# Turning the feed-forward's rows in 32 by 32 squares on VectorE, by way of DRAM, in a hybrid decoder layer

## The chip, the cores and the metric

One Trainium2 chip, of which the kernel uses one core. The metric is the time of one execution on the device in microseconds. The engines are written as in the profile: PE (TensorE, matmuls; PEld is its weight load), DVE (VectorE), ACT (ScalarE), POOL (GpSimd) and SP (SyncE, which here issues the DMAs). Each engine works through its own instructions in the order of the program; semaphores tie them together.

## The reference, cut to what matters

```python
SEQ = 1024; D_MODEL = 1024; D_FF = 4 * D_MODEL

def reference(x, ...):
    h = rmsnorm(x, mix_pre_norm)
    proj = h @ w_in
    ...
    mixed = jnp.concatenate([attn, rec], axis=-1) @ w_out
    x = x + rmsnorm(mixed, mix_post_norm)
    h = rmsnorm(x, mlp_pre_norm)
    ff = jnp.square(jax.nn.relu(h @ w_ff1)) @ w_ff2
    x = x + rmsnorm(ff, mlp_post_norm)
    return x
```

All is float32, with 1024 tokens. The change lies between `@ w_out` and `@ w_ff1`: the rows `h` of the second norm, with tokens on the partitions, have to be turned so that their 1024 features lie on the partitions, as the matmul with `w_ff1` needs them.

## The kernel before

The tokens are worked in NT = 8 blocks of 128 rows. A float32 matmul is made of three passes over a high and a low part of both operands (`three_pass`, lines 90 to 92, and the same in `mm1`, lines 1633 to 1635). `split_into` (86 and 87) makes the parts: ACT copies the high one (names ending in h), DVE subtracts it to get the low one (ending in l). This goes for weights too: `wl` is the low part of a block of FF1's weights, `wa2l` and `wa3l` are those of the second and third pair that FF1 starts with.

A loop over t = 0 to 7 runs the output projection: `late_out(t, 0)` and `late_out(t, 1)` are the matmuls `pwo<-…,mt` of block t. Work on earlier blocks is laid into the same loop by small tables. For a block r it is, in this order: `residual(r)` (DVE, lines 1274 and 1275: the new x, in `xres`, which an SP DMA also writes to DRAM as `x2d`, line 1293), POOL's factor of the norm (`x2r`), `residual_b(r)` (DVE, line 1303: x times factor times gain; the result, the row block of h, lies in `esum` for blocks 0 to 3, in place in `xres` for block 4 and in `x2n` for blocks 5 to 7), and the turn.

The turn is `next_turn(r)`: eight transposes on PE by the identity into two PSUM banks `ph` (line 1313) and two evacuations by ACT (line 1319) into `hraw[kh, th]`. Here kh is the half of the features and th the half of the tokens, so each of the four `hraw` tiles takes parts of four blocks. `TURN_MID` and `TURN_END` say at which t a block is turned. Blocks 6 and 7 come within FF1: `mm1(1, 1, …)` and `mm1(1, 2, …)` call `next_turn` between their matmuls.

`split_tokens` splits the turned tokens of th = 0 into `h2h` and `h2l`, tokens 0 to 255 at t = 5 and 256 to 511 at t = 7. FF1 works by products of halves: `mm1(q, p)` is product p of weight pair q. Products 1 and 2 use th = 0 alone; the others use sums with th = 1 (`B220l`, `T10l` and their like), which are made behind `wa3l` on DVE. FF1 begins with `mm1(0, 1)`, `mm1(1, 1)`, `mm1(0, 2)`, `mm1(1, 2)`, then products 1 of pairs 2 and 3 (`f12a`, `f13a`). Ahead of it SP issues the loads of raw weights: `wr2` and `wr3` (`early_load`) and four `w1r`.

SP issues nearly all DMAs, in order: one that waits for its data holds up all that stand behind it.

Of the kernel before, what the change touches and what calls it, by code (L numbers as in the profile page):

```python
# [8 lines left out]
F32 = mybir.dt.float32  # L9
F32R = mybir.dt.float32r  # L10
# [7 lines left out]
P = 128  # L18
T = 1024
D = 1024  # L20
NK = D // P
NT = T // P
# [15 lines left out]
def hymba_layer(ctx, tc, x, w_in, w_out, w_ff1, w_ff2, g_pre, lb_logits, g_mix, g_post,  # L38
                g_mlp, g_mlp_post, bias_tab, level_masks, ident_in, fold_in, out):
    nc = tc.nc  # L40
    V, S, G, TE = nc.vector, nc.scalar, nc.gpsimd, nc.tensor
# [4 lines left out]
    wide = ctx.enter_context(tc.tile_pool(name="wide", bufs=8))  # L46
# [3 lines left out]
    dp = ctx.enter_context(tc.tile_pool(name="spill", bufs=1, space=DRAM))  # L50

    def slab(tag, name, dtype=F32, shape=(P, T)):
        return sp.tile(list(shape), dtype, tag=tag, name=name,
                       bufs={"S": 9, "T": 9, "P": 3, "BT": 2, "V8": 2, "R": 1}[tag])

    def bank(tag, name):
        return ps.tile([P, 512], F32, tag=tag, name=name,
                       bufs={"mm": 2, "s": 2, "t": 2, "pv": 2}[tag])

    def half(name, dtype=F32):  # L60
        return sp.tile([P, 512], dtype, tag="half", name=name, bufs=2)

    def col(name, n=1):
        return tp.tile([P, n], F32, tag=f"c{n}", name=name)
# [15 lines left out]
    def rsqrt_mean(dst, ssum, n, width):  # L80
        t = col("ms", width)
        G.tensor_scalar(t, ssum, 1.0 / n, EPS, op0=ALU.mult, op1=ALU.add)
        G.tensor_tensor(out=dst, in0=t, in1=nhalf[:, :width], op=ALU.pow)
# [172 lines left out]
    pick32 = cp.tile([P, 32], F32, name="pick32")  # L256
    mix_dram = dp.tile([T, D], F32, name="mixd")
    x2_dram = [dp.tile([P, D], F32, name=f"x2d{t}") for t in range(NT)]

    def ig_evac(hd, pm, blocks):  # L260
        for u, t in enumerate(blocks):
            S.activation(hd["inat"][:, t], pm[:, u, 0], AF.Copy, scale=rstd0[:, t:t + 1])
            V.tensor_scalar(hd["gate"][:, t], pm[:, u, 1], rstd0[:, t:t + 1], None, op0=ALU.mult)
# [873 lines left out]
    rows, xress, mts, pmo, gains, scales = {}, {}, {}, {}, {}, {}  # L1137
# [24 lines left out]
    def early_sum(t):  # L1162
        return early["sum"][t // 2][:, t % 2]
# [82 lines left out]
    def x_again(t):  # L1246
        xress[t] = slab("P", f"xres{t}")
        nc.sync.dma_start(out=xress[t], in_=x[t * P:(t + 1) * P, :])

    def mixed_half(t, hf):  # L1250

        if hf == 0:
            scales["mix", t] = col("pss", 2)
        src = pmo[t, hf]
        if t < NE:
            whole = early_sum(t)[:, hf * 512:hf * 512 + 512]
            V.scalar_tensor_tensor(whole, src, scales["row", t], whole, op0=ALU.mult, op1=ALU.add)
            src = pmo[t, hf] = whole
        S.activation(half(f"dp{t}{hf}"), src, AF.Square, accum_out=scales["mix", t][:, hf:hf + 1])
        if hf == 1:  # L1260
            s2 = scales.pop(("mix", t))
            s1 = col("ps1")
            rp = scales["mix", t] = tp.tile([P, 1], F32, tag="prp", name=f"prp{t}", bufs=2)
            G.tensor_tensor(out=s1, in0=s2[:, 0:1], in1=s2[:, 1:2], op=ALU.add)
            rsqrt_mean(rp, s1, D, 1)

    def residual(t):
        xr = xress[t]
        rp = scales.pop(("mix", t))
        for hf in range(2):  # L1270
            sl = slice(hf * 512, hf * 512 + 512)
            src = pmo.pop((t, hf))
            add = src if t < NE else half(f"ad{t}{hf}")
            V.scalar_tensor_tensor(add, src, rp, gains["gpost"][:, sl], op0=ALU.mult, op1=ALU.mult)
            V.tensor_tensor(out=xr[:, sl], in0=add, in1=xr[:, sl], op=ALU.add)
            if t not in SQ_LATER:
                residual_sq(t, hf)
        if t not in SQ_LATER:
            residual_sq(t, 2)
# [17 lines left out]
    def residual_b(t):  # L1297
        xr = xress[t]
        if t < NE:
            xress[t] = early_sum(t)  # L1300
        elif t >= NT - 3:
            xress[t] = slab("S", f"x2n{t}")
        V.scalar_tensor_tensor(xress[t], xr, scales.pop(("x2", t)), gains["gmlp"], op0=ALU.mult, op1=ALU.mult)

    def next_turn(t):

        xr = xress.pop(t)
        th, c = t // 4, (t % 4) * P
        for kh in range(2):
            pt = bank("t", f"ph2{t}_{kh}")  # L1310
            for j in range(4):
                k = kh * 4 + j
                TE.transpose(pt[:, j * P:(j + 1) * P], xr[:, k * P:(k + 1) * P], ident)
            src = pt.rearrange("p (j c) -> p j c", j=4)
            if t % 4 == 0:
                hraw[kh, th] = wide.tile([P, 4, 512], F32, tag="A", name=f"hraw{kh}{th}")
                if th == 0:
                    h2[kh] = tuple(wide.tile([P, 4, 512], F32R, tag="A", name=f"h2{q}{kh}") for q in "hl")
            S.activation(hraw[kh, th][:, :, c:c + P], src, AF.Copy)

    def split_tokens(kh, c):

        hi, lo = (q[:, :, c:c + 2 * P] for q in h2[kh])
        split_into(hi, lo, hraw[kh, 0][:, :, c:c + 2 * P])
# [50 lines left out]
    for s in range(n_steps):  # L1375
# [19 lines left out]
        kind, g = ITEMS[i]  # L1395
# [51 lines left out]
    h2, hraw = {}, {}  # L1447
# [3 lines left out]
    SCALE = {3: (0,), 4: (1,), 5: (2,), 6: (4,), 7: (5,)}  # L1451
    SCALE_MID = {7: (6,)}
    SCALE_END = {5: (3,)}
    TURN_MID = {6: (3,)}
    TURN_END = {3: (0,), 4: (1,), 5: (2,), 6: (4,), 7: (5,)}

    def scaled(r):
        residual_b(r)
        if r + 3 < NT and r != 4:
            x_again(r + 3)  # L1460

# [5 lines left out]
    for t in range(NT):  # L1467
        late_out(t, 0, last_rows if t == 0 else None)
        for r in SCALE.get(t, ()):
            scaled(r)  # L1470
        if t > 0 and t + 1 < NT:
            for which in range(t + 1 < NE, 2):
                row_turn(t + 1, which, True)
            if t + 4 < NT:
                row_load(t + 4)
        for r in RES_END.get(t - 1, ()):
            for part_ in range(3):
                residual_sq(r, part_)
        if t < 2:
            x_again(t + 1)  # L1480
        if NE <= t + 2 < NT:
            row_attn(t + 2)
        if t in (5, 7):
            for kh in range(2):
                split_tokens(kh, (t - 5) * P)
        for r in RES.get(t, ()):
            residual(r)
        for r in TURN_MID.get(t, ()):
            next_turn(r)
        mixed_half(t, 0)  # L1490
        late_out(t, 1)
        for r in SCALE_MID.get(t, ()):
            scaled(r)
        if t == NT - 1:
            w_get(W10 + 1, 0)
        for r in TURN_END.get(t, ()):
            next_turn(r)
            if r == 4:
                x_again(7)
        if t + 3 < NT:  # L1500
            row_norm(t + 3)
        if t == 4:
            w_get(W10, 0)
        mixed_half(t, 1)
        for r in RES_END.get(t, ()):
            residual(r)
        for r in SCALE_END.get(t, ()):
            scaled(r)

# [110 lines left out]
    def mm1(q, p, bank_key, first, mid=None, at=0):  # L1622
        if first:
            pb[q, bank_key] = banks.get(f"f1{q}{bank_key}")
        pm = pb[q, bank_key]
        w, b = ops1[q][p], bops[RHS[p]]
        for k in range(4):
            if mid is not None and k == at:
                mid()
            lhs = tuple(x[:, k * P:(k + 1) * P] for x in w)  # L1630
            rhs = part_of(b, k)
            st, sp_ = first and k == 0, k == 3
            TE.matmul(pm, lhs[0], rhs[0], start=st, stop=False, skip_group_check=True)
            TE.matmul(pm, lhs[0], rhs[1], start=False, stop=False, skip_group_check=True)
            TE.matmul(pm, lhs[1], rhs[0], start=False, stop=sp_, skip_group_check=True)
# [18 lines left out]
    def out_p1(q):  # L1654
        S.activation(x_of(q, 0), pb[q, "a"], AF.Copy)

    def out_p2(q, dst=None):
        r = half(f"rl{q}")
        dst = lay[q]["E1"][:, 0] if dst is None else dst
        S.activation(r, pb[q, "a"], AF.Relu)  # L1660
        if q < FIRST:
            S.activation(dst, r, AF.Square)
        else:
            V.scalar_tensor_tensor(dst, pb[q, "a"], 0.0, r, op0=ALU.max, op1=ALU.mult)
        drop(pb.pop((q, "a")))
# [124 lines left out]
    mm1(0, 1, "a", True)  # L1790
    out_p1(0)
    residual(NT - 1)
    mm1(1, 1, "a", True, lambda: next_turn(NT - 2), 1)
    out_p1(1)
    small.add("S")
    residual_b(NT - 1)
# [3 lines left out]
    early_load(4)  # L1800
    mm1(0, 2, "a", False)
    out_p2(0)
    for tag in ("T", "BT"):
        small.add(tag)
    mm1(1, 2, "a", False, lambda: next_turn(NT - 1), 2)
# [430 lines left out]
    for i in range(4):  # L2236
        t = 4 + i
# [100 lines left out]
```

## Time and profile before

| | us |
|---|---|
| median of 3 runs | 1190.43 (1189.83 to 1190.44) |
| the profiled execution | 1190.04 |
| its span, first to last instruction | 1188.1 |
| first turn (block 0) on PE | 518.33 |
| first matmul of FF1 | 569.90 |
| last turn (block 7) on PE | 580.45 |
| granted clock of PE, mean | 0.998 |

A row of a timeline has a start in us from the start of the span, a duration, the engine, the line in the kernel, the operation, out<-in by the program's names (without numbers of buffers), the shape and how many such instructions stand in the row; at the end, in brackets, how long the engine stood idle ahead of it and what ended that. "SPq" is the DMA queue of SP; its rows tell when a DMA was issued. A row of DMA issues gives the count, the size of one, and the median time from issue to landing. A matmul's duration includes the pipeline, so the step from one start to the next tells what it costs.

### The profile page before, as it was taken

Reading aid. Unit: us, or ns where it says so; the run is one execution under the profiler, and the core shown is the slowest. Engines: PE = TensorE matmul, PEld = TensorE weight load, DVE = VectorE, ACT = ScalarE, POOL = GpSimd, SP = SyncE. Lnnn points to the kernel's source line nnn. Section 1 sums busy time; section 2 is a strip of 40 time slices with the busy share of each in tenths; the row PEclk is TensorE's granted clock in tenths of the full one; section 3 lists DMA queues with packets and bytes.
Section 4 is the critical chain, followed back from the end, with each engine's and each line's share of the span. In section 5 each row is a group of like instructions: output and inputs, shape, how many; then the busy total and the mean of one; then the engine's idle time right before and its main releaser. Section 6 shows DMA issues by size and latency. Waiting matters only on the chain.

```text
span 1188.1 us, 17598 instructions
## 1 busy us (share of the span) xinstructions
PE 1178.1 (99%) x6486; PEld 1004.2 (85%) x6486; DVE 839.9 (71%) x1428; ACT 548.9 (46%) x1082; POOL 294.3 (25%) x282
## 2 busy tenths in 40 slices
PE   9999999999999999999999999999999999999997
PEld 9898989878888888888888888888888888888886
DVE  5686969686666667577697666675686653588796
ACT  7633424343666677764654222222244544434562
POOL 0112122001111010252503775667540000000022
PEclk9999999999999999999999999999999999999999
DMA  5222323147453644452425465554587524433337
GB/s 221 71 69 86 98 86 99 48 114 185 103 148 95 170 128 126 157 192 89 168 89 201 158 225 180 184 177 167 196 328 274 176 90 157 162 95 101 109 104 283
DMA packets 90549, 175.49 MB, mean 148 GB/s; under 512 B 14944, under 2 KB 42464, under 8 KB 90464
## 3 DMA queue, kind: packets, MB, share of 16 engines
q1 hardware_dynamic: 90320, 174.37, 45.4%
q8 instruction: 51, 0.84, 0.3%
q14 instruction: 34, 0.28, 0.1%
q10 hardware_dynamic: 144, 0.00, 0.0%
HBM read 116.91 MB, written 47.99 MB: 139 GB/s over the span
## 4 chain that ended last, share of the span: by engine, by line
PE 92%; ACT 3%; DVE 3%; issue 1%; DMA 0%; POOL 0%; DVEq 0%; POOLq 0%; ACTq 0%
PE f L2078 18%; PE f2s L2078 7%; PE pig L90 3%; PE pig L92 2%; PE pig L91 2%; PE pwo L90 2%; PE pwo L92 2%; PE pwo L91 2%; PE pl L536 1%; PE pm_ak L90 1%; PE pm_ak L92 1%; PE pm_ak L91 1%; PE pm_av L90 1%; PE pm_av L92 1%; PE pm_f L90 1%
## 5 line engine op out<-in xcount | busy, mean ns | idle before, releaser
L87 DVE TENSOR_TENSOR al<-ar,ah 128x1024 fp32r<-128x1024 f32 x56 | 70.7, 1262 | 79.7 <-ACT ah L86 77.4
L2078 PE MATMUL f<-bh,ah 128*128 128x512 f32 x320 | 124.5, 389 | 0.0
L2078 PE MATMUL f<-bl,ah 128*128 128x512 f32 x320 | 124.5, 389 | 0.0
L2078 PE MATMUL f<-bh,al 128*128 128x512 f32 x320 | 124.5, 389 | 0.0
L86 ACT ACTIVATE ah<-ar 128x1024 fp32r<-128x1024 f32 x56 | 59.1, 1056 | 86.8 <-DMA ar<-actd 86.4
L2078 PEld LDWEIGHTS f<-bh,ah 128*128 128x128 f32 x320 | 60.1, 188 | 12.6
L2078 PEld LDWEIGHTS f<-bl,ah 128*128 128x128 f32 x320 | 60.1, 188 | 12.5
L2078 PEld LDWEIGHTS f<-bh,al 128*128 128x128 f32 x320 | 60.1, 188 | 12.3
L2152 POOL TENSOR_SCALAR lbl<-ssq 128x1 f32<-128x1 f32 x4 | 3.3, 822 | 245.0 <-ACT fd L2148 244.8
L1701 POOL TENSOR_TENSOR e<-x,e 128x512 f32<-128x512 f32 x14 | 21.6, 1541 | 131.7 <-DVE x L1652 131.7
L2078 PE MATMUL f2s<-bh,al 128*128 128x512 f32 (+1 forms) x128 | 48.9, 382 | 0.0
L2078 PE MATMUL f2s<-bl,ah 128*128 128x512 f32 (+1 forms) x128 | 48.9, 382 | 0.0
L2078 PE MATMUL f2s<-bh,ah 128*128 128x512 f32 (+1 forms) x128 | 48.9, 382 | 0.0
L710 POOL TENSOR_SCALAR tout<-traw 128x256 f32<-128x256 f32 x16 | 19.2, 1199 | 103.0 <-DMA traw<-in_bias_tab_dram 100.2
L87 DVE TENSOR_TENSOR bl<-br,bh 128x1024 fp32r<-128x1024 f32 x32 | 40.1, 1255 | 1.1 <-ACT bh L86 1.0
L2095 ACT ACTIVATE acc<-f 128x512 f32<-128x512 f32 x28 | 16.7, 598 | 48.8 <-PE f L2078 48.8
L86 ACT ACTIVATE bh<-br 128x1024 fp32r<-128x1024 f32 x32 | 33.6, 1050 | 4.0 <-PE f L2078 3.0
L758 POOL TENSOR_TENSOR kl<-kf,kh 64x512 fp32r<-64x512 f32 x12 | 16.2, 1348 | 74.9 <-ACT kh L757 74.9
L90 PE MATMUL pwo<-woh,mt 128*128 128x512 f32 x80 | 32.2, 403 | 0.0
L87 DVE TENSOR_TENSOR wl<-raw,wh 128x1024 fp32r<-128x1024 f32 x21 | 25.7, 1224 | 8.6 <-ACT wh L86 8.6
L92 PE MATMUL pwo<-woh,mt 128*128 128x512 f32 x80 | 31.3, 391 | 0.0
L91 PE MATMUL pwo<-wol,mt 128*128 128x512 f32 x80 | 31.2, 390 | 0.0
(1725 smaller groups left out, 3882.7 us busy)
## 6 DMA issues: line engine op xcount, KB each, us to landing
ar<-actd SPq DMA_DIRECT2D x56, 512.0 KB, 3.6
br<-in_w_ff_dram SPq DMA_DIRECT2D x16, 1024.0 KB, 5.8
raw<-in_w_in_dram SPq DMA_DIRECT2D x28, 512.0 KB, 3.9
w1r<-in_w_ff_dram SPq DMA_DIRECT2D x14, 1024.0 KB, 6.4
actd<-e SPq DMA_DIRECT2D x17, 768.0 KB, 4.2
actd<-e SPq DMA_DIRECT2D x11, 1024.0 KB, 4.1
xr<-in_x_dram SPq DMA_DIRECT2D x8, 512.0 KB, 8.1
raw<-in_w_out_dram SPq DMA_DIRECT2D x8, 512.0 KB, 3.9
```

The lines of the kernel that those rows point to most:

```text
L86: S.activation(hi, src, AF.Copy)
L87: eng.tensor_tensor(out=lo, in0=src, in1=f32(hi), op=ALU.subtract)
L90: TE.matmul(dst, lhs[0], rhs[0], start=start, stop=False)
L91: TE.matmul(dst, lhs[0], rhs[1], start=False, stop=False)
L92: TE.matmul(dst, lhs[1], rhs[0], start=False, stop=stop)
L536: TE.matmul(pl[a:b, n, :96], kt[:, (4 * u + n) * P + a:(4 * u + n) * P + b], qs[:, :, 32 * g:32 * g + 32], start=True, stop=True, skip_gro ...
L710: G.tensor_scalar(by_class(dst[:, part_ * w:(part_ + 1) * w]), in_blocks(raw[:, FAR * DIL:]), 8.0, None, op0=ALU.mult)
L758: G.tensor_tensor(out=kl[a:b], in0=src, in1=f32(kh[a:b]), op=ALU.subtract)
L1701: eng[0].tensor_tensor(out=e1[:, 3], in0=a21, in1=e1[:, 2], op=ALU.add)
L2078: TE.matmul(pm, a[:, j, c], b[:, j, d], start=start and j == 0 and q == 0, stop=stop and j == 1 and q == 2, skip_group_check=True)
L2095: S.activation(acc_at(p, i), pm, AF.Copy)
L2152: G.tensor_scalar(base[:, t:t + 1], sums[j][:, t:t + 1], 1.0 / D, EPS, op0=ALU.mult, op1=ALU.add)
```

## The change

For blocks 0 to 6, the turn on PE and ACT goes. In its place:

- `scaled(r)` (and so each `residual_b` of blocks 0 to 6) is followed by an SP DMA that writes the block to DRAM, `x2nd` (128 by 1024, 512 KB);
- `lay_out(r)` reads it back into the same tile by four SP DMAs, one for each 32 partitions, so that the squares of 32 by 32 elements lie where they have to be after the turn. Each piece is 32 elements (128 bytes) and each DMA has 1024 of them (128 KB);
- `square_turn(r)` turns it by two DVE instructions, each of which turns 32 by 32 squares (128 x 4 x 128 elements), straight from the tile into `hraw`.

The tables set the place of `lay_out` and of `square_turn` apart. The first half of `split_tokens` moves from t = 5 to t = 6. Block 7 is turned by `next_turn` as before.

```diff
+    def raw_room(t):
+        ...
+    def lay_out(t):
+
+        src = x2n_dram[t].rearrange("(a r) (k g f) -> g r k a f", a=4, g=4, f=32)
+        for g in range(4):
+            nc.sync.dma_start(out=xress[t][32 * g:32 * g + 32].rearrange("p (k a f) -> p k a f", k=NK, a=4), in_=src[g])
+
+    def square_turn(t):
+
+        xr = xress.pop(t)
+        th, c = t // 4, (t % 4) * P
+        raw_room(t)
+        for kh in range(2):
+            V.transpose(hraw[kh, th][:, :, c:c + P], xr[:, kh * 512:kh * 512 + 512].rearrange("p (k c) -> p k c", k=4))
+        if t == 4:
+            x_again(7)
...
-    TURN_MID = {6: (3,)}
-    TURN_END = {3: (0,), 4: (1,), 5: (2,), 6: (4,), 7: (5,)}
+    LAY_MID = {6: (3,)}
+    LAY_END = {3: (0,), 4: (1,), 5: (2,), 6: (4,), 7: (5,)}
+    TURN_MID = {4: (0,), 5: (1,), 6: (2,), 7: (4,)}
+    TURN_END = {6: (3,)}
 
     def scaled(r):
         residual_b(r)
+        nc.sync.dma_start(out=x2n_dram[r], in_=xress[r])
...
-        if t in (5, 7):
+        if t in (6, 7):
             for kh in range(2):
-                split_tokens(kh, (t - 5) * P)
+                split_tokens(kh, (t - 6) * 2 * P)
         for r in RES.get(t, ()):
             residual(r)
+        for r in LAY_MID.get(t, ()):
+            lay_out(r)
+        mixed_half(t, 0)
         for r in TURN_MID.get(t, ()):
-            next_turn(r)
-        mixed_half(t, 0)
+            square_turn(r)
         late_out(t, 1)
...
-        for r in TURN_END.get(t, ()):
-            next_turn(r)
-            if r == 4:
-                x_again(7)
+        for r in LAY_END.get(t, ()):
+            lay_out(r)
...
         for r in SCALE_END.get(t, ()):
             scaled(r)
+        for r in TURN_END.get(t, ()):
+            square_turn(r)
...
     residual(NT - 1)
-    mm1(1, 1, "a", True, lambda: next_turn(NT - 2), 1)
+    lay_out(NT - 2)
+    square_turn(NT - 3)
+    mm1(1, 1, "a", True)
...
     out_p2(0)
+    square_turn(NT - 2)
```

DVE's instructions from the last part of t = 6 to the start of FF1, before. `ad5`, `xres5` are residual(5), `x2n5` is residual_b(5), `h2l` the split of tokens 256 to 511; then the same for block 6, and the weights' low part `wl37`:

```order
L1275 TENSOR_TENSOR xres5_6288<-ad51_6427,xres5_6288 128x512
L1303 SCALAR_TENSOR_TENSOR x2n5_6528<-xres5_6288,x2r5_6433,gmlp_5804 128x1024
L87 TENSOR_TENSOR h2l0_6091<-hraw00_6089,h2h0_6090 128x4x256
L87 TENSOR_TENSOR h2l1_6100<-hraw10_6098,h2h1_6099 128x4x256
L1274 SCALAR_TENSOR_TENSOR ad60_6534<-pwo6_0_6380,prp6_6498,gpost_5802 128x512
L1275 TENSOR_TENSOR xres6_6378<-ad60_6534,xres6_6378 128x512
L1274 SCALAR_TENSOR_TENSOR ad61_6540<-pwo6_1_6454,prp6_6498,gpost_5802 128x512
L1275 TENSOR_TENSOR xres6_6378<-ad61_6540,xres6_6378 128x512
L1303 SCALAR_TENSOR_TENSOR x2n6_6580<-xres6_6378,x2r6_6546,gmlp_5804 128x1024
L87 TENSOR_TENSOR wl37_6583<-raw37_5785,wh37_6582 128x1024
```

The same stretch in the changed kernel, from the end of residual(5) to the split of tokens 256 to 511:

```order
L1276 TENSOR_TENSOR xres5_6284<-ad51_6419,xres5_6284 128x512
L1326 STREAM_TRANSPOSE hraw00_6197<-esum1_5158 128x4x128
L1326 STREAM_TRANSPOSE hraw10_6200<-esum1_5158 128x4x128
L1326 STREAM_TRANSPOSE hraw00_6197<-esum1_5158 128x4x128
L1326 STREAM_TRANSPOSE hraw10_6200<-esum1_5158 128x4x128
L1304 SCALAR_TENSOR_TENSOR x2n5_6504<-xres5_6284,x2r5_6425,gmlp_5811 128x1024
L87 TENSOR_TENSOR h2l0_6199<-hraw00_6197,h2h0_6198 128x4x256
L87 TENSOR_TENSOR h2l1_6202<-hraw10_6200,h2h1_6201 128x4x256
```

The turns of block 2 and block 3 (both lie in `esum1`) stand between residual(5) and residual_b(5). The turn of block 4 stands between residual(6) and residual_b(6) in the same way, and behind it `wl37`.

On SP, at the head of FF1, before:

```order
L1293 DMA x2d6_140<-xres6_6378 128x1024
L1770 DMA wr2_6618<-in_w_ff1_dram 128x1024
L1770 DMA wr3_6620<-in_w_ff1_dram 128x1024
L1789 DMA w1r00_6622<-in_w_ff1_dram 128x1024
L1789 DMA w1r01_6623<-in_w_ff1_dram 128x1024
L1789 DMA w1r10_6626<-in_w_ff1_dram 128x1024
L1789 DMA w1r11_6627<-in_w_ff1_dram 128x1024
L1293 DMA x2d7_141<-xres7_6493 128x1024
```

And in the changed kernel, where `x2nd` is the block's copy in DRAM and a row "32x32x32 x4" is one lay_out:

```order
L1294 DMA x2d6_140<-xres6_6365 128x1024
L1249 DMA xres7_6536<-in_x_dram 128x1024
L1482 DMA x2nd6_148<-x2n6_6563 128x1024
L1318 DMA x2n5_6504<-x2nd5_147 32x32x32 x4
L1796 DMA wr2_6594<-in_w_ff1_dram 128x1024
L1796 DMA wr3_6596<-in_w_ff1_dram 128x1024
L1815 DMA w1r00_6598<-in_w_ff1_dram 128x1024
L1815 DMA w1r01_6599<-in_w_ff1_dram 128x1024
L1815 DMA w1r10_6602<-in_w_ff1_dram 128x1024
L1815 DMA w1r11_6603<-in_w_ff1_dram 128x1024
L1294 DMA x2d7_141<-xres7_6536 128x1024
L1318 DMA x2n6_6563<-x2nd6_148 32x32x32 x4
```

Four DMAs more stand between x2d6 and the loads of weights (the load of xres7, which moved behind x2d6, x2nd6 and lay_out(5)), and lay_out(6) follows the loads and x2d7. The lay_out of block 3 stands on SP behind x2d5:

```order
L1482 DMA x2nd3_145<-esum1_5158 128x1024
L1249 DMA xres6_6365<-in_x_dram 128x1024
L1482 DMA x2nd4_146<-xres4_6147 128x1024
L1294 DMA x2d5_139<-xres5_6284 128x1024
L1318 DMA esum1_5158<-x2nd3_145 32x32x32 x4
L1318 DMA xres4_6147<-x2nd4_146 32x32x32 x4
```

DVE in the changed kernel behind residual(7), where `x2n5` and `x2n6` are blocks 5 and 6:

```order
L1326 STREAM_TRANSPOSE hraw01_6532<-x2n5_6504 128x4x128
L1326 STREAM_TRANSPOSE hraw11_6533<-x2n5_6504 128x4x128
L1304 SCALAR_TENSOR_TENSOR x2n7_6658<-xres7_6536,x2r7_6632,gmlp_5811 128x1024
L87 TENSOR_TENSOR wa2l_6661<-wr2_6594,wa2h_6660 128x1024
L1326 STREAM_TRANSPOSE hraw01_6532<-x2n6_6563 128x4x128
L1326 STREAM_TRANSPOSE hraw11_6533<-x2n6_6563 128x4x128
L87 TENSOR_TENSOR wa3l_6708<-wr3_6596,wa3h_6707 128x1024
L87 TENSOR_TENSOR B220l_6739<-hraw11_6533,B220h_6738 128x1024
```

Before, `wa3l` stood right behind `wa2l`; now the turn of block 6 stands between them.

More of the change, by code (lines that the diff above doesn't have):

```diff
@@ L258, in hymba_layer @@
     x2_dram = [dp.tile([P, D], F32, name=f"x2d{t}") for t in range(NT)]
+    x2n_dram = [dp.tile([P, D], F32, name=f"x2nd{t}") for t in range(NT - 1)]
     def ig_evac(hd, pm, blocks):
@@ L1303, in residual_b @@
         V.scalar_tensor_tensor(xress[t], xr, scales.pop(("x2", t)), gains["gmlp"], op0=ALU.mult, op1=ALU.mult)
+    def raw_room(t):
+        th = t // 4
+        if t % 4 == 0:
+            for kh in range(2):
+                hraw[kh, th] = wide.tile([P, 4, 512], F32, tag="A", name=f"hraw{kh}{th}")
+                if th == 0:
+                    h2[kh] = tuple(wide.tile([P, 4, 512], F32R, tag="A", name=f"h2{q}{kh}") for q in "hl")
+    def lay_out(t):
[6 more added lines that the diff above has]
+        raw_room(t)
+        for kh in range(2):
+            V.transpose(hraw[kh, th][:, :, c:c + P], xr[:, kh * 512:kh * 512 + 512].rearrange("p (k c) -> p k c", k=4))
+        if t == 4:
+            x_again(7)
     def next_turn(t):
@@ L1314, in next_turn @@
             src = pt.rearrange("p (j c) -> p j c", j=4)
[L1315 to L1318, printed above, removed]
             S.activation(hraw[kh, th][:, :, c:c + P], src, AF.Copy)
```

## Prediction, made before the changed kernel was run

> **What bounds the kernel now.** I read the head of the page first, then the chain of work that ended last, then the timelines of the engines around the place that is changed.
>
> ```profile
> span 1188.1 us, 17598 instructions
> PE 1178.1 (99%) x6486; PEld 1004.2 (85%) x6486; DVE 839.9 (71%) x1428; ACT 548.9 (46%) x1082; POOL 294.3 (25%) x282
> PE 92%; ACT 3%; DVE 3%; issue 1%; DMA 0%; POOL 0%; DVEq 0%; POOLq 0%; ACTq 0%
> ```
>
> PE is busy for 99% of the span and carries 92% of the chain. The list of PE's waits, cut to 500 to 1188 us, has no row at all: from the change onwards PE never waits. So each microsecond of PE work taken out there shortens the run, and each microsecond for which PE is made to wait there lengthens it, since there is no later wait that could absorb it. The sum is therefore kept at PE.
>
> The profiled execution took 1190.04 us (span 1188.1 and 1.94 around it); the median of the timed runs, 1190.43, lies 0.03% above. I add to 1190.04.
>
> **What is removed.** PE's timeline in block 0 and at the head of FF1 (start, duration, and what it does):
>
> ```profile
> 518.10 0.40 PE L92 MATMUL pwo<-woh,mt 128*128 128x512 f32 x1
> 518.33 1.04 PE L1313 MATMUL ph<-ident,esum 128*128 128x128 f32 x8
> 519.12 0.47 PE L90 MATMUL pwo<-woh,mt 128*128 128x512 f32 x1
> 519.44 0.39 PE L91 MATMUL pwo<-wol,mt 128*128 128x512 f32 x1
> ...
> 569.11 1.03 PE L1313 MATMUL ph<-ident,x2n 128*128 128x128 f32 x8
> 569.90 0.48 PE L1633 MATMUL f10a<-h2h,w1h 128*128 128x512 f32 x1
> ...
> 573.17 0.40 PE L1635 MATMUL f11a<-h2h,wl 128*128 128x512 f32 x1
> 573.40 1.04 PE L1313 MATMUL ph<-ident,x2n 128*128 128x128 f32 x8
> ...
> 576.36 0.39 PE L1633 MATMUL f10a<-h2h,w1h 128*128 128x512 f32 x1
> ...
> 585.87 0.39 PE L1635 MATMUL f13a<-h2h,wa3l 128*128 128x512 f32 x1
> ```
>
> From one matmul start to the next is 0.23 us. From 518.10 to 519.44 there are two such steps (0.46) and the eight transposes: 1.34 - 0.46 = 0.88 us for a block. Seven blocks lose them: 7 x 0.88 = **6.2 us** of PE. Six of the seven lie ahead of mm1(0,1), so without any wait that product would start at 569.90 - 5.3 = 564.6, and the third matmul of mm1(1,1), the first that needs `wl`, at 573.17 - 5.3 = 567.9. The 14 evacuations on ACT go too, which nothing waited for at PE.
>
> **What a turned block costs now.** Each block is written to DRAM (512 KB), read back by four transfers of 1024 pieces of 128 bytes (128 KB each), and turned by two instructions on DVE. The trace has no 128-byte pieces alone, so I bound their price by windows of the DMA view:
>
> ```profile
> DMA packets 328, 0.00 MB, mean 1 GB/s; under 512 B 328, under 2 KB 328, under 8 KB 328
> q1 hardware_dynamic: 328, 0.00, 17.5%
> ...
> DMA packets 562, 0.08 MB, mean 80 GB/s; under 512 B 511, under 2 KB 562, under 8 KB 562
> q1 hardware_dynamic: 562, 0.08, 52.8%
> ...
> DMA packets 1428, 0.69 MB, mean 172 GB/s; under 512 B 81, under 2 KB 1428, under 8 KB 1428
> q1 hardware_dynamic: 1428, 0.69, 76.6%
> ...
> DMA packets 1398, 4.27 MB, mean 356 GB/s; under 512 B 288, under 2 KB 416, under 8 KB 1397
> q1 hardware_dynamic: 1397, 4.25, 89.5%
> ...
> mixd<-anat SPq DMA_DIRECT2D x12, 128.0 KB, 2.4
> ```
>
> The share is of 16 engines' time. In 423 to 424 us, pieces of a few bytes: 0.175 x 16 / 328 = 8.5 ns each. In 466 to 467, pieces of 142 bytes in the mean (80 KB / 562): 0.528 x 16 / 562 = 15.0 ns. In 274 to 278, pieces of about 500 bytes: 0.766 x 64 / 1428 = 34.3 ns. I take **15 ns**, the row nearest in size, and keep 8.5 and 34.3 for the range. A block has 4096 pieces, 256 for each of 16 engines: 3.84 us (2.2 to 8.8). In 8 to 20 us, 4.25 MB took 0.895 x 12 us, 396 GB/s: a transfer of 512 KB takes 1.3 us. A transfer of 128 KB in pieces of 512 bytes lands after 2.4 us, of which 16 x 34.3 ns are pieces: about 1.85 us is latency. So a block lands 5.7 us after its first issue.
>
> A rule speaks against the middle value. The Trainium skill, "DMA: Bandwidth & Descriptors", Specifications, puts the smallest transfer that runs at line rate at 512 bytes and says that below it the engine reads, modifies and writes. Taken as a price, it would make a 128-byte piece no cheaper than one of 512, and the sum below 1214.5 instead of 1199.7; this case's trace disagrees for smaller pieces, at 8.5 against 34.3 ns.
>
> For the transposes I take a DVE row of equal size, `xres<-ad,xres` 128x512 at 0.69 us (0.65 from start to start in a row): 1.3 us a block. The ends are nothing, and 1.8 times that, since the same instruction L1303 takes 1.29 us at 557.58 and 2.31 at 577.72, while POOL is busy.
>
> **Where it is late: block 3.** DVE's and SP's timelines of before:
>
> ```profile
> 554.86 0.69 DVE L1275 TENSOR_TENSOR xres<-ad,xres 128x512 f32<-128x512 f32 x1
> 557.58 1.29 DVE L1303 SCALAR_TENSOR_TENSOR x2n<-xres,x2r,gmlp 128x1024 f32<-128x1024 f32 x1 [2.03 <-POOL x2r L83]
> 560.59 2.36 DVE L87 TENSOR_TENSOR h2l<-hraw,h2h 128x1024 fp32r<-128x1024 f32 x2 [1.72 <-ACT h2h L86]
> ...
> 565.16 0.69 DVE L1275 TENSOR_TENSOR xres<-ad,xres 128x512 f32<-128x512 f32 x1
> 567.88 1.29 DVE L1303 SCALAR_TENSOR_TENSOR x2n<-xres,x2r,gmlp 128x1024 f32<-128x1024 f32 x1 [2.03 <-POOL x2r L83]
> 569.08 1.22 DVE L87 TENSOR_TENSOR wl<-raw,wh 128x1024 fp32r<-128x1024 f32 x1
> ...
> 577.72 2.31 DVE L1303 SCALAR_TENSOR_TENSOR x2n<-xres,x2r,gmlp 128x1024 f32<-128x1024 f32 x1 [2.04 <-POOL x2r L83]
> ...
> 583.15 1.34 DVE L87 TENSOR_TENSOR wa3l<-wr,wa3h 128x1024 fp32r<-128x1024 f32 x1 [0.90 <-ACT wa3h L86]
> 587.20 2.28 DVE L87 TENSOR_TENSOR B220l<-hraw,B220h 128x1024 fp32r<-128x1024 f32 x1 [2.70 <-ACT B220h L86]
> ```
>
> ```profile
> 555.58 0.32 SPq L1293 DMA_DIRECT2D x2d<-xres  x1
> ...
> 565.88 0.32 SPq L1293 DMA_DIRECT2D x2d<-xres  x1
> 566.25 4.42 SPq L1770 DMA_DIRECT2D wr<-in_w_ff_dram  x2
> 570.71 1.98 SPq L1789 DMA_DIRECT2D w1r<-in_w_ff_dram  x4
> 575.71 0.33 SPq L1293 DMA_DIRECT2D x2d<-xres  x1
> ```
>
> Blocks 0, 1 and 2 have about one whole t-step (10 us: the three x2d issues lie that far apart) between their lay_out and their turn: 5.7 us fit in, and I cost them at nothing. Block 3 doesn't have it. On SP its lay_out stands behind x2d5, which waits for residual(5), and on DVE its turn stands right behind residual(5) and block 2's. I leave the end of residual(5) at 555.55: PE's earlier work would move it forward by some 2.6 us, but the first pair of h2l splits (2 x 1.22 us), formerly at 540.4 in t = 5, now stands ahead of it:
>
> ```profile
> L87 DVE TENSOR_TENSOR h2l<-hraw,h2h x4: 1218/1220/1225, 540.4 to 561.7; 128x1024 fp32r<-128x1024 f32 x4
> ```
>
> Then x2d5 is issued at 555.6, lay_out(3) at 556.0, and it lands at 561.7. DVE stands still until then (from 556.9, after block 2's turn), and everything queued behind is late: block 3's turn to 563.0, residual_b(5) 1.29 to 564.3, two h2l 2.36 to 566.7, residual(6) 2.9 (before, from the splits' end at 562.95 to 565.85) to 569.6, POOL's factor 2.03 and residual_b(6) 1.29 to 572.9, block 4's turn within the 2.03, `wl` 1.22 to **574.1**, where before it was ready at 570.3. PE wants it at 567.9 and stands still for 6.2 us. mm1(1,1) then ends 573.17 to 576.36 less 0.88 behind it, 574.1 + 2.3 = 576.4: what the transposes gave is spent, to 0.04 us.
>
> **Where it is later still: block 6.** Its write to DRAM needs residual_b(6) at 572.9. Behind that write, on SP and so in the transfers' queue, stand lay_out(5), the two `wr` loads and the four `w1r` loads of FF1's weights (all 512 KB), x2d7, and only then lay_out(6): 1.3 + 3.84 + 6 x 1.3 + 1.3 + 3.84 = 18.1 us. That lay_out(6) lands at 572.9 + 18.1 + 1.85 = **592.9** at the latest in this reckoning; x2d7 itself could be issued at 577, far ahead of its turn in the queue. Block 6's turn takes until 594.2. Behind it on DVE stands `wa3l` (1.34 us, a copy of weights that has nothing to do with block 6): 595.5. PE needs wa3l for the third matmul of mm1(3,1), at 585.87 before. It comes 9.6 us later. A smaller wait ahead of it, block 7's transposes for a residual_b(7) that stands behind block 5's turn (about 2 us), lies inside these 9.6.
>
> Behind wa3l the other splits of DVE follow (B220l, which began at 587.20, starts at 595.5, 8.3 later, while PE is 9.6 later), so no further wait is added, and none is there to give anything back. Sum: 1190.04 + 9.6 = **1199.7** us. The mean busy share of the DMA engines, in tenths for 40 slices of 29.7 us:
>
> ```profile
> DMA  5222323147453644452425465554587524433337
> ```
>
> The 512 KB writes of blocks 0 to 5 cost at most an SP issue (0.32 us) and 1.3 us of transfer time each, in slices that are a half, a fifth and two fifths busy (5, 2, 4, from 505 to 594 us); without that cover block 3 would land 1.3 later.
>
> Ends: with 8.5 ns each lay_out is 1.65 us shorter; block 3 and block 6 bring that once each, and lay_out(5) in the queue once: 1199.7 - 5 = 1194.7. With 34.3 ns each is 5 us longer: 1214.5. Turns at nothing: 2.6 less (1197.1); at 1.8 times: 2.1 more (1201.8).
>
> **Rivals.** (1) *Everything hides*: no wait takes the place of the transposes, and all 6.2 us stay: 1190.04 - 6.2 = 1183.9, faster. For it: PE waits for nothing, and the DMA engines are half idle there. Its point is sharp: wl must be ready by 567.9, so lay_out(3) landed by 555.5, before it can be issued in the order of SP; and lay_out(6) by 577. It needs residual(5) some 6 us earlier than I put it and transfers that don't line up behind the loads. Chance 0.10, half-way cases included.
>
> (2) *The loads don't hold lay_out(6)*: its pieces run between the loads', and it lands 5.7 us after x2d7 is issued at 577, at 583. Turn and wa3l end at 585.7, in time for 585.87. Then block 3's wait alone counts, which took the saving: about 1190.0, the same. Against it: the four w1r loads, issued in one row, land in the median only as a queue would let them. Chance 0.12.
>
> ```profile
> w1r<-in_w_ff_dram SPq DMA_DIRECT2D x4, 512.0 KB, 5.7
> x2d<-xres SPq DMA_DIRECT2D x8, 512.0 KB, 3.7
> ```
>
> Four in a row take 5.7 us where one takes 3.7.
>
> (3) *Small pieces cost as large ones* (34.3 ns): block 3 lands 5 us later, wl is ready at 579.0; residual_b(6) at 577.8, lay_out(6) at 577.8 + 28.0 + 1.85 = 607.7, wa3l at 610.3: 24.4 later than 585.87, 1214.5. Against it the 15.0 ns of the middle row. Chance 0.08.
>
> **How the numbers follow.** The forecast has 0.70, the rivals 0.10, 0.12 and 0.08. About 0.2% (2.4 us) is what a measurement of this kernel can tell from no change. Slower: 0.70 + 0.08 = 0.78; same 0.12; faster 0.10. The range begins at 1188.0, so that rival 2 is in it, and ends at 1206.0, above the ends of the transposes' cost and two fifths of the way to the dear end of the pieces; left out are rival 1, rival 3 and little of the forecast.
>
> **What would show it.** PE's waits after 500 us, empty before, should have two main rows: one on DVE's wl (about 6 us), one on wa3l (about 7). DVE should stand still before block 3's turn (4.8 us, put down to the DMA of lay_out(3)) and before block 6's (over 5). lay_out's time to landing should be near 3 us for the first of four and 5.7 for the last, and over 10 for block 6. If block 6's turn waits less than 2 us, rival 2 holds and the loads were no obstacle; if block 3's turn doesn't wait, rival 1 does. A turn far from 0.65 us for each instruction, or a lay_out far from 3.8 us, moves the sum by the amounts above and leaves the mechanism.

## The result, and the profile after

| | before | changed |
|---|---|---|
| median, us | 1190.41 (1189.83 to 1190.44, 4 runs) | 1202.64 (1201.55 to 1204.26, 4 runs) |
| profiled execution, us | 1190.04 | 1202.70 |
| its span, us | 1188.1 | 1200.9 |
| ratio of the runs | | 1.0105, 95% interval 1.0093 to 1.0118 |

The changed kernel is slower by 12.2 us, 1.05%. The forecast was 9.6 us slower.

PE's list of waits, cut to 500 to 1201 us, had no row before. Now it has five (what waits, for what, total us, count, longest):

```profile
PE f13a L1661 <- DVE wa3l L87: 7.1, 1, 7.1
PE f11a L1659 <- ACT wh L86: 3.6, 1, 3.6
PE ph L1338 <- DVE x2n L1304: 1.5, 1, 1.5
PE f11a L1661 <- DVE wl L87: 0.9, 1, 0.9
PE f10a L1660 <- DVE h2l L87: 0.4, 1, 0.4
```

Together they are 13.5 us. The second, fourth and fifth belong to block 3, the third (block 7's transposes, which wait for x2n) to block 5, and the first to block 6. DVE's list of waits, cut to 550 to 606 us, has two rows on the read-back of a block:

```profile
DVE hraw L1326 <- DMA x2n<-x2nd: 12.1, 2, 8.8
DVE hraw L1326 <- DMA esum<-x2nd: 5.2, 1, 5.2
```

Both stand ahead of turns (L1326), and it is the landing of a lay_out that ends them: 5.2 us for block 3, 3.3 for block 5 and 8.8 for block 6. Blocks 0, 1, 2 and 4 have no such wait, here or in the list from 500 us on. The timeline of DVE around blocks 3 and 6, and that of SP:

```profile
555.59 1.30 DVE L1326 STREAM_TRANSPOSE hraw<-esum 128x512 f32<-128x512 f32 x2
562.07 1.31 DVE L1326 STREAM_TRANSPOSE hraw<-esum 128x512 f32<-128x512 f32 x2 [5.18 <-DMA esum<-x2nd]
...
572.94 1.22 DVE L87 TENSOR_TENSOR wl<-raw,wh 128x1024 fp32r<-128x1024 f32 x1
...
593.61 1.30 DVE L1326 STREAM_TRANSPOSE hraw<-x2n 128x512 f32<-128x512 f32 x2 [8.76 <-DMA x2n<-x2nd]
594.84 1.61 DVE L87 TENSOR_TENSOR wa3l<-wr,wa3h 128x1024 fp32r<-128x1024 f32 x1
```

```profile
555.70 0.32 SPq L1294 DMA_DIRECT2D x2d<-xres  x1
556.11 3.12 SPq L1318 DMA_DIRECT2D esum<-x2nd  x4
...
573.05 0.32 SPq L1482 DMA_DIRECT2D x2nd<-x2n  x1
573.48 3.84 SPq L1318 DMA_DIRECT2D x2n<-x2nd  x4
577.36 1.48 SPq L1796 DMA_DIRECT2D wr<-in_w_ff_dram  x2
578.88 2.10 SPq L1815 DMA_DIRECT2D w1r<-in_w_ff_dram  x4
581.07 0.38 SPq L1294 DMA_DIRECT2D x2d<-xres  x1
581.50 9.59 SPq L1318 DMA_DIRECT2D x2n<-x2nd  x4
```

Block 3: x2d5 at 555.7 (forecast 555.6), landed at 562.0 (561.7), wl ready at 574.2 (574.1). Block 6: landed at 593.6 (592.9), wa3l ready at 596.45 (595.5). All of these hold 0.35 us that the trace was late already ahead of the change (see below). The four issues of lay_out(6), the last row, took 9.6 us, since SP itself was held in two of them. The chain of what ended last shows it (start, length, what):

```profile
577.36 4.83 DMA wr<-in_w_ff_dram
...
582.21 3.83 SPq L1318
...
586.08 4.28 SPq L1318
...
590.41 3.18 DMA x2n<-x2nd
```

This hold by itself is not what makes block 6 late: in the run with large pieces below, the four issues end at 581.95, and the data still comes only at 589.9, behind the loads.

What the forecast did not have is behind the waits. PE's clock, from the table of stretches (us; busy us of PE, PEld, DVE, ACT and POOL with counts; then PE's granted clock, DMA share, GB/s):

```profile
572.00:577.40 5.40, 4.41 (x10) 3.03 (x11) 4.51 (x6) 1.83 (x6) 1.97 (x3) 0.51 0.76 234
577.40:583.00 5.60, 4.89 (x22) 3.72 (x20) 2.29 (x4) 2.00 (x4) 0.93 (x3) 1.00 1.02 281
...
596.50:601.00 4.50, 4.50 (x11) 3.54 (x12) 3.30 (x2) 0.45 (x1) 1.08 (x1) 0.50 0.01 2
601.00:606.00 5.00, 5.00 (x23) 4.19 (x22) 3.25 (x3) 3.72 (x5) 0.00 (x0) 0.98 0.00 0
```

In about the 5 us after each of the two long waits PE was granted half its clock, and the matmuls ran in steps of 0.43 us:

```profile
596.50 0.80 PE L1661 MATMUL f13a<-h2h,wa3l 128*128 128x512 f32 x1 [7.08 <-DVE wa3l L87]
597.10 0.63 PE L1659 MATMUL f13a<-h2h,wa3h 128*128 128x512 f32 x1
597.52 0.63 PE L1660 MATMUL f13a<-h2l,wa3h 128*128 128x512 f32 x1
```

At 0.2 us a step over its usual 0.23, I count 2.3 us lost in each stretch. The account of the profiled execution, 12.66 us longer: -6.2 for the transposes, +13.5 of waits, +4.6 of slow steps make 11.9. A further 0.35 us was there before the change begins; the same transpose in the kernel before (first row) and in the changed one:

```profile
508.80 0.49 PE L1208 MATMUL pmt<-ident,row 128*128 128x128 f32 x3
509.15 0.49 PE L1209 MATMUL pmt<-ident,row 128*128 128x128 f32 x3
```

The last 0.4 us are not assigned. This transpose stands ahead of everything that was changed, and in the twelve traces of this document it starts between 508.68 and 510.86: traces of different kernels differ by up to 2.2 us before any change acts, so a trace's time is compared with another's only with this offset taken off.

### The profile page after: what moved, and what is told of

Read it like the earlier page. It is cut to its first block, busy times and chain, and to the rows that moved or that the text cites. A ratio compares the mean times of both kernels' runs of the same rounds, so it can differ in the third digit from the quotient of the medians.

```text
span 1200.9 us, 17546 instructions
## 1 busy us (share of the span) xinstructions
PE 1176.6 (98%) x6430; PEld 1000.7 (83%) x6430; DVE 844.3 (70%) x1442; ACT 541.8 (45%) x1068; POOL 293.6 (24%) x282
## 4 chain that ended last, share of the span: by engine, by line
PE 86%; DVE 5%; ACT 3%; issue 2%; DMA 1%; SPq 1%; POOL 1%; DVEq 0%; POOLq 0%; ACTq 0%
PE f L2107 18%; PE f2s L2107 7%; PE pig L90 2%; PE pig L92 2%; PE pig L91 2%; PE pwo L90 1%; PE pwo L92 1%; PE pwo L91 1%; PE pm_ak L90 1%; PE pm_ak L92 1%; PE pl L537 1%; PE pm_ak L91 1%; SPq L1318 1%; PE pm_av L90 1%; PE pm_av L92 1%
```

## Experiments

In each, all that isn't named is as in the changed kernel ("before_wait…": as in the kernel before). Each ratio is against the kernel before, run on the same chip.

**Block 6 back on PE**, and not written to DRAM either.

```diff
-        nc.sync.dma_start(out=x2n_dram[r], in_=xress[r])
+        if r < NT - 2:
+            nc.sync.dma_start(out=x2n_dram[r], in_=xress[r])
...
-    lay_out(NT - 2)
     square_turn(NT - 3)
-    mm1(1, 1, "a", True)
+    mm1(1, 1, "a", True, lambda: next_turn(NT - 2), 1)
...
     out_p2(0)
-    square_turn(NT - 2)
```

> Block 6 is turned by PE again, inside mm1(1,1); blocks 0 to 5 stay as in the changed kernel. Theory: the 7.1 us for which PE waits for wa3l are block 6's alone (its lay_out lies behind the weight loads), and the slow matmul steps behind that wait (0.43 us instead of 0.23, about 2 us) go with it. What stays is block 3's wait: mm1(1,1) ended 1.7 us later than before, and 0.88 us of transposes come back, so about 1190.04 + 2.6 = 1192.6 us, and no wait for wa3l in the trace. Rival: the cost is spread over all blocks (small pieces and DVE's turns as such), each a seventh of the 12.3 us: about 1200.9.

Measured: 1193.69 us, ratio 1.0025 (1.0014 to 1.0036). Two waits are left:

```profile
PE f11a L1660 <- ACT wh L86: 3.6, 1, 3.6
PE f11a L1662 <- DVE wl L87: 1.4, 1, 1.4
```

The wait for wa3l is gone, and 9 us with it. The cost is not spread over the blocks: block 6 alone bears 9.0 of the 12.2 us.

**lay_out(3) ahead of residual(5).**

```diff
-        for r in RES.get(t, ()):
-            residual(r)
         for r in LAY_MID.get(t, ()):
             lay_out(r)
+        for r in RES.get(t, ()):
+            residual(r)
```

> As the changed kernel, but lay_out(3) stands ahead of residual(5), and so ahead of x2d5 on SP. Theory: DVE's 5.2 us of standing still before block 3's turn go, wl and residual_b(6) come about 5 us earlier, PE's waits for wh, wl and h2l (4.9 us) shrink to about 1 us. Block 6's write and lay_out move 5 us forward with it, the loads still lie ahead of it, so wa3l comes at about 591.5 instead of 596.5, and the total falls by about 5 us: 1197.7. Rival: DVE is late by its own work (the turns and the splits moved into t = 6) and not by the landing: wl stays near 574 and the total near 1202.6.

Measured: 1198.55 us, ratio 1.0066 (1.0051 to 1.0081). Block 3's turn now waits 0.57 us for its data instead of 5.18, PE's waits for wh and h2l are gone, and that for wl is 1.3:

```profile
PE f13a L1661 <- DVE wa3l L87: 9.3, 1, 9.3
PE ph L1338 <- DVE x2n L1304: 1.4, 1, 1.4
PE f11a L1661 <- DVE wl L87: 1.3, 1, 1.3
```

So block 3 was late by its landing, not by DVE's work. PE arrives earlier at f13a and waits there longer, since block 6 moved by less than PE did.

**Both together**, that is all edits of the two runs above, and block 5's turn behind wa2l:

```diff
-    lay_out(NT - 2)
-    square_turn(NT - 3)
-    mm1(1, 1, "a", True)
+    mm1(1, 1, "a", True, lambda: next_turn(NT - 2), 1)
...
     out_p2(0)
-    square_turn(NT - 2)
+    square_turn(NT - 3)
```

> Both: block 6 on PE, lay_out(3) ahead of residual(5), and block 5's turn placed behind wa2l so that residual_b(7) does not stand behind it. Theory: with both waits gone six blocks' transposes are saved, 5.3 us, less about 1.2 us in which PE still waits for wl: 1190.04 - 4.1 = 1186.0 us, faster than both kernels. Rival: the turned blocks cost something else that no wait shows (DVE, SP or transfers): 1190 or above.

Measured: 1188.50 us (1187.44 to 1190.60, 10 runs), ratio 0.9984 (0.9975 to 0.9994): faster than the kernel before, by 2.0 us instead of 4. That is 0.16%, below the 0.2% that the prediction took as the least that can be told from no change, though the interval leaves out 1. The profiled execution, the fastest of the ten, has 0.7 us of waiting for wl and 0.4 for x, and a granted clock of 0.999. What the slower ones spent, no trace shows; an offset ahead of the change, as in the twelve traces above, would be large enough for most of it.

**The w1r loads behind lay_out(6).**

```diff
-        for f in range(2):
-            nc.sync.dma_start(out=flat(q_raw[q][f]), in_=w_ff1[2 * q + f])
     mm1(0, 1, "a", True)
     out_p1(0)
     residual(NT - 1)
     lay_out(NT - 2)
+    for q in range(2):
+        for f in range(2):
+            nc.sync.dma_start(out=flat(q_raw[q][f]), in_=w_ff1[2 * q + f])
```

> As the changed kernel, but the four w1r loads are issued behind lay_out(6). Theory: they take 4 x 1.3 us of the transfers' queue ahead of lay_out(6), so it lands 5.2 us earlier, at about 588.4 instead of 593.6, and PE's wait for wa3l shrinks from 7.1 to about 2 us. The total falls to about 1195.4 if nothing else turns late; the sums that POOL makes of the w1r weights start some 8 us later and may take part of it back. Rival: lay_out(6) is late by its own pieces or by its issue on SP, not by the loads ahead of it: it lands at 593 as before.

Measured: 1200.23 us, ratio 1.0082 (1.0066 to 1.0099). Block 6's turn begins at 589.56 instead of 593.61, so lay_out(6) landed about 4 us earlier, and the wait for wa3l halves:

```profile
PE f13a L1661 <- DVE wa3l L87: 3.4, 1, 3.4
...
PE f10c L1661 <- DVE wf01l L87: 0.5, 1, 0.5
```

The loads do hold lay_out(6). The total gained only 2.4 of the 4. POOL's sums start at 591.98 instead of 586.24, and DVE stands still for 5.0 us for the split of their result, wf01; PE waits 0.5 there. The slow stretch behind the wait of 3.4 stayed (1.7 us lost). So the total was forecast too low: the loads gave 4 us and not 5.2, and the clock behind the wait that is left was not in it.

**The kernel before with a wait put in.** wa3l is written four times more, with the same values:

```diff
         ops1[q] = {"A": split_pair(f"wa{q}", raw)}
+        for _ in range(4 if q == 3 else 0):
+            V.tensor_tensor(out=flat(ops1[q]["A"][1]), in0=flat(raw), in1=f32(flat(ops1[q]["A"][0])), op=ALU.subtract)
```

> The kernel before, with the low part wa3l written four more times on DVE (the same values), so that PE has to wait for it at mm1(3,1), with no turn, lay_out or extra transfer anywhere. A write takes 1.3 to 2.3 us there, so wa3l ends some 8 us later and PE should wait about 7 us. Theory: a wait of that length costs more than itself, since the matmuls behind it run at half rate (0.43 us a step) for some 4 us: about 10 matmuls x 0.2 = 2 us more than the wait in the trace, total about 1190.04 + 7 + 2.2 = 1199. Rival: the slow steps come from the small transfers or from DVE's turns next to them; here they are missing, and the total rises by the wait alone, about 1197.

Measured: 1200.66 us, 10.3 over the kernel before, ratio 1.0083 (1.0068 to 1.0098), with one wait of 7.4 us. The table of stretches behind it:

```profile
594.90:599.30 4.40, 4.40 (x10) 3.49 (x11) 3.27 (x2) 0.00 (x0) 1.06 (x1) 0.50 0.02 4
599.30:604.00 4.70, 4.70 (x22) 3.89 (x21) 2.86 (x3) 3.72 (x5) 0.00 (x0) 0.98 0.00 0
```

Half the clock, with no turn in squares and no lay_out in the kernel: the wait alone brings it. The medians put the price at 2.9 us over the wait's length. The trace gives the surer figure, 2.2 us in slow steps: its execution is 11.1 us longer than that of the kernel before, 7.4 of it the wait, 2.2 the slow steps and 1.5 an offset ahead of the change (the transpose at 508.80 starts at 510.30).

**The same with one more write instead of four.**

> As the kernel before with wa3l written four more times, but written only once more: wa3l ends about 2.3 us later and PE waits for it about 1 us. Theory (slow steps follow only a wait of more than about 2 us): no matmul behind it at 0.43 us, and the total rises by the wait alone, to about 1191.3. Rival: any wait there brings the slow stretch: about 1193.5.

Measured: 1191.26 us, 0.9 over the kernel before, ratio 1.0007 (0.9998 to 1.0017). PE waited 0.7 us, and the clock behind it is 1.00:

```profile
587.00:592.00 5.00, 4.95 (x22) 4.08 (x23) 4.53 (x3) 3.71 (x5) 4.92 (x3) 1.00 0.02 3
```

A wait of 0.7 us cost itself, to 0.2 us.

**PE kept busy during the waits.**

```diff
         w, b = ops1[q][p], bops[RHS[p]]
+        for u in range({(1, 1): 14, (3, 1): 28}.get((q, p), 0)):
+            w_, k_ = ops1[q - 1][p], u % 4
+            TE.matmul(pm, w_[0][:, k_ * P:(k_ + 1) * P], part_of(b, k_)[0], start=True, stop=True, skip_group_check=True)
```

> The changed kernel, with 14 matmuls that nothing reads put ahead of mm1(1,1) and 28 ahead of mm1(3,1), so that PE works for 3.2 and 6.4 us of the two long waits (3.6 and 7.1 us). Their results are overwritten by the product itself. Theory: the slow matmul steps follow from PE standing still; with what is left of each wait below 1.5 us they don't come, and the total falls by about 2.3 + 2.3 us to about 1198.0, though PE does more work. Rival: the slow steps have another cause at that time: the total stays near 1202.6.

Measured: 1201.21 us, ratio 1.0090 (1.0077 to 1.0104), 1.4 below the changed kernel and not 4.6. The expectation held at the first wait and failed at the second:

```profile
571.50:577.00 5.50, 4.10 (x17) 3.10 (x18) 4.61 (x6) 1.74 (x5) 1.97 (x3) 1.00 0.98 254
...
595.30:600.00 4.70, 4.70 (x14) 3.71 (x15) 3.31 (x2) 1.30 (x3) 1.10 (x1) 0.64 0.01 2
```

In mm1(1,1), where 0.4 and 1.4 us of waiting were left, the clock stayed full. At the other, 2.0 us were left, more than I had reckoned with, and although nearly 12 us of matmuls without a wait stood ahead of it, that was enough for a slow stretch of its own. The 1.4 us gained are not the clock's in the main: wa3l itself was ready 1.2 us earlier (595.25), and the slow stretch behind it cost 1.7 us instead of 2.3. The expectation also counted the first stretch's 2.3 us as a gain, which it could not be in the total, since PE waits for wa3l behind it.

**Large pieces.** The same bytes in rows of 4 KB; the order of the squares is left out, so this kernel computes something else.

```diff
-            nc.sync.dma_start(out=xress[t][32 * g:32 * g + 32].rearrange("p (k a f) -> p k a f", k=NK, a=4), in_=src[g])
+            nc.sync.dma_start(out=xress[t][32 * g:32 * g + 32], in_=x2n_dram[t][32 * g:32 * g + 32])
```

> The changed kernel, with lay_out as four transfers of the same 128 KB in whole rows of 4 KB instead of squares' rows of 128 bytes; the order of the squares is left out, so that the output is not the reference's. Theory: a lay_out takes 1.3 instead of about 3.7 us of transfers and issue, so block 3 lands about 2.6 us earlier, lay_out(6) about 8 (three lay_outs are in its way, block 3's, block 5's and its own); wa3l comes at about 588.5 instead of 596.5 and the total is about 1194.5; the wait for wa3l is still there, about 4 us, because the loads still lie ahead. Rival (small pieces cost as much as large ones, or next to nothing beside latency): no change.

Measured: 1199.32 us, ratio 1.0078 (1.0064 to 1.0091): 3.3 below the changed kernel, where the theory had 8. Block 3 waited 4.6 us instead of 5.2, block 6 8.3 instead of 8.8, and PE's wait for wa3l was 5.9 us instead of 7.1:

```profile
555.69 2.14 SPq L1317 DMA_DIRECT2D esum<-x2nd  x4
...
561.04 1.30 DVE L1325 STREAM_TRANSPOSE hraw<-esum 128x512 f32<-128x512 f32 x2 [4.57 <-DMA esum<-x2nd]
...
578.74 3.21 SPq L1317 DMA_DIRECT2D x2n<-x2nd  x4
...
589.92 1.30 DVE L1325 STREAM_TRANSPOSE hraw<-x2n 128x512 f32<-128x512 f32 x2 [8.32 <-DMA x2n<-x2nd]
```

For block 3 it took 5.35 us from first issue to turn, against 5.96 with small pieces. The small pieces are a minor part: the four issues, the transfer ahead and the latency remain. The theory's step "a lay_out is mostly transfer time" falls. Block 6's four issues are done at 581.95 here, not held as in the changed kernel, and its data still comes 8 us later. So the loads ahead of it hold it in the transfers, not SP's issue.

**Reordered.** Block 6 on PE and lay_out(3) early as above; the split that makes wl, block 5's lay_out and turn, and block 6's transposes each get another place:

```diff
-    LAY_END = {3: (0,), 4: (1,), 5: (2,), 6: (4,), 7: (5,)}
+    LAY_END = {3: (0,), 4: (1,), 5: (2,), 6: (4,), }
...
+        if t == NT - 1:
+            w_get(W10 + 1, 0)
         for r in SCALE_MID.get(t, ()):
             scaled(r)
-        if t == NT - 1:
-            w_get(W10 + 1, 0)
...
             nc.sync.dma_start(out=flat(q_raw[q][f]), in_=w_ff1[2 * q + f])
+    lay_out(NT - 3)
     mm1(0, 1, "a", True)
...
     mm1(1, 1, "a", True, lambda: next_turn(NT - 2), 3)
...
     early_split(3)
+    square_turn(NT - 3)
```

> Six blocks by squares, as in the run with lay_out(3) ahead of residual(5), and further: the split that makes wl stands ahead of residual_b(6), block 6's transposes on PE come at the last quarter of mm1(1,1), and block 5's lay_out stands behind the weight loads, its turn behind wa3l. Theory: the three small waits that were left there (0.7 us for wl, and 0.4 us and two shorter ones at the products behind POOL's sums, whose weights had been loaded later) go, and the six blocks' 5.3 us stay but for a few tenths: about 1185.3 us. Rival: what is missing from the 5.3 is not in these waits: 1187 to 1189 as in that run.

Measured: 1187.13 us, ratio 0.9972 (0.9960 to 0.9983): faster than the kernel before by 0.28%, the best of the study together with the next run, though not 1185.3. The profiled execution, the fastest of the six at 1186.30, is 3.7 us under that of the kernel before; with its two waits that makes 5.1 of the 5.3 us. One new wait of 1.0 us took the place of an old one:

```profile
PE f11a L1660 <- ACT x L1682: 1.0, 1, 1.0
PE f11a L1662 <- DVE wl L87: 0.4, 1, 0.4
```

**Reordered, with block 6's transposes one product later** (`mm1(0, 2, "a", False, lambda: next_turn(NT - 2), 2)` instead of in `mm1(1, 1, …)`).

> As the reordered kernel with six blocks by squares, but block 6's transposes on PE move from the end of mm1(1,1) into mm1(0,2), so that ACT's evacuations of block 6 no longer stand ahead of its evacuation of mm1(1,1)'s product. Theory: PE's wait of 1.0 us for that evacuation goes, the rest stays: about 1186.2 us. Rival: ACT is held by the squares' sums of residual(7) instead, and the wait and the 1187.1 us stay.

Measured: 1187.16 us, ratio 0.9973 (0.9962 to 0.9984), no change. The wait for ACT's x is gone, and one for block 7's x2n of 0.5 us came, with smaller gaps beside it. The rival had the time right, but not its reason; what sets the time now is not shown.

## Why the prediction was right, and by how much it was short

The side was right, and the mechanism; the size was short, since the price of a wait in PE's clock was left out. Step by step:

- *Six of seven blocks' transposes are saved ahead of FF1, 0.88 us each*: right. FF1's first matmul came at 564.94, and less the 0.35 us of offset that is 564.59, where the forecast had 564.6:

```profile
564.94 0.39 PE L1659 MATMUL f10a<-h2h,w1h 128*128 128x512 f32 x1
```

  With block 6 on PE and block 3 early, 2.0 to 3.2 us of the 5.3 reach the end in the medians, and waits account for part of the rest.
- *Blocks 0, 1, 2 and 4 cost nothing*: right, no wait of DVE for their landing.
- *Block 3 is late behind x2d5, and the saving goes*: right, shown by moving its lay_out (4.1 us). wl came at 574.2 (forecast 574.1). PE stood still not for wl first but for wh, 3.6 us; ACT makes wh behind residual(6)'s sums, and so it was late by the same landing.
- *A lay_out takes 3.84 us of transfers and 1.85 of latency*: the sum was right (5.7 forecast, 5.96 measured from first issue to turn), the split was not. The 128-byte pieces cost less than the 15.0 ns that I took; the row behind that figure mixed 511 pieces under 512 bytes with 51 larger ones, so its 142 bytes are the mean of unlike pieces. From 560 to 562 us, with nothing else in transfer, 1.048 x 2 x 16 us / 2603 = 12.9 ns each:

```profile
DMA packets 2603, 0.33 MB, mean 164 GB/s; under 512 B 2603, under 2 KB 2603, under 8 KB 2603
## 3 DMA queue, kind: packets, MB, share of 16 engines
q1 hardware_dynamic: 2603, 0.33, 104.8%
```

  That is 3.3 us a block. The issues on SP take nearly as long, 0.78 us each (3.12 for four at 556.11), and the last one lands 3.5 us after its issue begins, behind the 512 KB of x2d5, which the forecast left out. The rival of 34.3 ns a piece disagrees with this row. So does the rule of the Trainium skill ("DMA: Bandwidth & Descriptors", Specifications), line rate from 512 bytes up, when it is read as a price of a piece; as to the rate the trace agrees with it, 164 GB/s here against 396 for the large loads of the prediction.
- *lay_out(6) behind the loads*: right, shown from both sides (block 6 on PE: 9 us less; w1r behind it: landed 4 us earlier). It landed 0.7 us later than forecast, and that it came so close is partly luck: the pieces were cheaper (3.3 instead of 3.84 us, twice), and the large transfers dearer. From 581 to 589 us, with few small pieces, 372 GB/s were moved: 1.4 us for 512 KB instead of the 1.3 that the sum has eight times. By this estimate the two errors, 1.1 and 0.9 us, nearly cancel. The signs for landing were off as well: from a DMA's own issue the lay_outs took 3.1 to 9.6 us, where the prediction had 5.7 for the last of four and over 10 for block 6.
- *wa3l late by 9.6, and nothing behind it*: here is the shortfall, a term left out. The matmul with wa3l came at 596.50, 10.6 us later than before and 1.0 later than forecast, and then the slow stretch cost another 2.3. 10.6 + 2.3 = 12.9, against 12.66 for the whole execution. The sum had taken the wait at its own length. So the forecast was short by a fifth of the loss. The first slow stretch cost nothing in the end: PE had to wait for wa3l anyway, and without it would have waited 2.3 us longer.

The Trainium skill, "TensorE: Matmul & The Clock Gate", "What's actually happening", describes a clock gate that halves PE's clock after an idle window of about 3.4 us and gives it back after as long a busy one. The trace agrees as to the half (0.50 and 0.51) and roughly as to the length (the slow steps lasted 4.8 and 5.3 us). It disagrees where a wait of 2.0 us was enough. As an estimate from the page's 3.4 us, half of them lost behind the wait for wa3l would have added 1.7 us to the forecast, 1201.4 in all.

Open: why the runs of the version with both waits removed spread over 3 us; whether there is a fixed length between 1.5 us (a wait in the changed kernel with a full clock behind it) and 2.0 us at which a wait turns expensive; and what sets the price, which does not follow the length of the wait. A wait of 9.3 us (lay_out(3) early) was followed by slow steps that cost 1.5 us, waits of 7.1 and 7.4 us by 2.3 and 2.2, and the two waits of 3.6 and 1.4 us with block 6 on PE by 3.2.

## What to carry to other kernels

Work taken off a saturated engine pays only where its replacement is ready in time, so follow each replaced piece through three places: what stands ahead of its transfer in the issuing engine's order, how long it takes to land, and what stands behind its consumer (here a split of weights behind block 6's turn). A piece that can't be ready is better left where it was: six moved blocks, with block 3's read-back issued early, beat seven by 14 us or more and none by 0.16 to 0.28%. Price a wait of a saturated PE of 2 us or more above its length, since its clock falls; in these traces that cost 1.5 to 3.2 us more.

## What the runs showed of the hardware that was not expected

- Each wait of PE from 2.0 us upwards (2.0 to 9.3 us, in seven kernels) was followed by a stretch of slow steps of 0.43 us, which cost 1.5 to 3.2 us beyond the wait (2.3 each time in the changed kernel). Waits of 0.7 to 1.5 us were not, unless a longer one stood just ahead.
- Matmuls put into a wait kept the clock up in mm1(1,1) (1.00 instead of 0.51).
- An issue of 1024 pieces on SP takes 0.78 us, against 0.32 for 128 large rows (x2d), and SP stood in such an issue for up to 4.3 us while earlier loads were under way; with 32 large rows in their place four issues took 3.2 us in all. Why it is held is not shown.
- DVE's turn of 128x512 in squares takes 0.65 us from start to start, as long as an add of that size (0.69 us each when measured to the end).
